# Value products of a banded attention: six of 256 columns in place of four of 512, with values and queries loaded by key head

## Chip, cores and metric

The kernel runs on one core of one Trainium2 chip. The metric is the device time of one execution in microseconds (us). The engines are named as in the profile: PE is TensorE (matrix products; PEld is its loading of weights), DVE is VectorE, ACT is ScalarE, POOL is GpSimd, SP is SyncE, which issues nearly all DMA transfers here. Each engine works through its own instructions in order, and waits where an instruction needs a result of another engine.

## What is computed

One layer of a decoder: an input projection, two branches (attention over a sliding window of 128 keys, and a chunked gating MLP), their merge, and a convolutional FFN. A prompt of 1024 tokens and 8 samples of 8 tokens share the weights. The change concerns the prompt's attention alone:

```python
BLOCK = WINDOW = 128; HEAD_DIM = 64; N_HEADS = 16; N_KV_HEADS = 4; GQA_GROUP = 4
def attn_prompt(q, k, v, sinks):
    ...                                     # blocks of 128 queries; keys of the block before and of the own one
    diff = arange(BLOCK)[:, None] + BLOCK - arange(2 * BLOCK)[None, :]
    band = (diff >= 0) & (diff < WINDOW)
    mask = band[None] & valid[:, None, :]
    o = sink_attention(qb, kk, vv, mask[:, None, None], sinks)   # softmax with a learned sink, then p @ v
```

For query q of a block the band lets in key j of the own block where j <= q, and key j of the block before where j > q. So each query sees 128 keys, one for each j.

## The kernel before

**Numbers in two parts.** Products run in a rounded 32-bit type (fp32r), and an operand x is held as a high part and a low part (`split`: the high part is a rounded copy by ACT, the low part the difference by DVE). A product is then three products, or, where the weights hold both parts side by side, two.

**Tokens in two groups.** Group 0 has the 64 sample tokens and prompt blocks 0 to 3, group 1 prompt blocks 4 to 7. `attention(gr, pieces)` runs for group 0, then for group 1. It has 16 steps, one for each key head `kv` (0 to 3) and block `i` (0 to 3); one step handles the 4 query heads that share the key head, 128 queries each: 512 columns.

**One step** has three parts, which the loop at the end of `attention` puts two steps apart:

- `sc_p`: scores by 8 products `sc` (two for each query head); `s` has 128 slots for each query, slot j holds the score of the key j that the band lets in; maximum, exponential and sum follow on DVE and ACT.
- `tr_p`: four transposes `pt` turn the probabilities over (slots on the partitions, 512 query columns); `ph` and `pl` are their high and low parts. POOL keeps the slots j <= q of each (`affine_select`) as `ch` and `cl`.
- `pv_p`: values. Tile `vst` of a block holds for each key head 64 columns of high and 64 of low parts of v. Four products of 512 columns add up in `po`: v of the block before times `ph` and `pl`, and `dvst` (v of the own block less v of the block before) times `ch` and `cl`, which corrects the slots whose key is in the own block. The very first block of the prompt (b = 0) has no block before it and takes two products only: so of 32 steps 28 have four.

**Work beside the attention.** Between these parts `fill()` calls the next pieces of other work: products `mm` of `branch` (group 0) or `merge` (group 1). They are what PE does while a step's chain of ACT, DVE and POOL runs. A scheduler orders every engine's instructions by priority when the program is built, so the rows of an engine stand near but not exactly in the order of the code.

**Values in DRAM.** Early in the program, `v_out` writes for each block a tile of values (`vd0` to `vd6`) and one of differences (`dvd1` to `dvd7`), 128 x 512 numbers each, from buffers `ws`. `prepare(gr)` returns the loads: per group 3 or 4 tiles `vst` and as many `dvst`, all key heads at once, which `fill()` issues near the beginning of the group's attention; keys `kst` and queries `q` are loaded for each key head by `operands(kv)`.

## Time and profile before

| | |
|---|---|
| median of 3 runs | 1527.02 us (1525.86 to 1528.16) |
| the profiled execution's own time | 1527.68 us |
| its span, first to last instruction | 1526.0 us, so 1.68 us lie around it |
| mean granted TensorE clock | 0.996 of full speed |
| PE, PEld busy | 1512.0 us (99%), 1489.0 us (98%) |
| DVE, ACT, POOL busy | 1152.4 us (76%), 822.6 us (54%), 257.3 us (17%) |
| DMA | 284.05 MB, mean 186 GB/s |

The steps of the prompt's attention lie between about 490 us and 690 us: group 0 up to 600 us, group 1 from there. Busy shares are of the span; products of PE overlap in the records (a record lasts from its start to its modelled end), so the time that one takes on PE is read from the distance between starts. A row of the timeline gives start, duration, engine, line, operation, the tiles written and read, and in square brackets how long the engine sat idle before it and for whom.

### The profile page before, as it was taken

Reading aid. Unit: us, or ns where it says so; the run is one execution under the profiler, and the core shown is the slowest. Engines: PE = TensorE matmul, PEld = TensorE weight load, DVE = VectorE, ACT = ScalarE, POOL = GpSimd, SP = SyncE. Lnnn points to the kernel's source line nnn. Section 1 sums busy time; section 2 is a strip of 40 time slices with the busy share of each in tenths; the row PEclk is TensorE's granted clock in tenths of the full one; section 3 lists DMA queues with packets and bytes.
Section 4 is the critical chain, followed back from the end, with each engine's and each line's share of the span. In section 5 each row is a group of like instructions: output and inputs, shape, how many; then the busy total and the mean of one; then the engine's idle time right before and its main releaser. Section 6 shows DMA issues by size and latency. Waiting matters only on the chain.

```text
span 1526.0 us, 31224 instructions
## 1 busy us (share of the span) xinstructions
PE 1512.0 (99%) x12158; PEld 1489.0 (98%) x12158; DVE 1152.4 (76%) x1910; ACT 822.6 (54%) x1744; POOL 257.3 (17%) x371
## 2 busy tenths in 40 slices
PE   9999999999999999999999999999999999999998
PEld 9999999999998989989999999999999999999997
DVE  6896778766544786888658888898899888785675
ACT  7565764554553675774433555555555556353562
POOL 0000002100020221330122211242232222000003
PEclk9999999999999999999999999999999999999998
DMA  8452458657559646729988432332243226973453
GB/s 289 160 194 89 176 199 263 200 187 246 199 204 297 230 160 208 253 88 307 329 292 279 143 120 97 117 143 97 82 151 111 77 93 217 359 259 96 127 175 132
DMA packets 126819, 284.05 MB, mean 186 GB/s; under 512 B 14800, under 2 KB 32016, under 8 KB 126672
## 3 DMA queue, kind: packets, MB, share of 16 engines
q1 hardware_dynamic: 122640, 278.52, 53.9%
q10 hardware_dynamic: 4032, 3.55, 0.7%
q8 instruction: 95, 1.56, 0.4%
q14 instruction: 52, 0.43, 0.1%
HBM read 193.40 MB, written 90.59 MB: 186 GB/s over the span
## 4 chain that ended last, share of the span: by engine, by line
PE 73%; DVE 4%; issue 3%; ACT 2%; DMA 2%; POOL 1%; POOLq 0%; SPq 0%; DVEq 0%; ACTq 0%
PE st L294 40%; PE mm L235 16%; PE dn L1666 11%; PE sc L1184 2%; PE po L1232 2%; PE pt L1211 1%; POOL x L1731 1%; DVE wl L41 1%; DMA wraw<-wt 1%; PE mx L831 1%; DMA s<-sd 1%; ACT s L1201 1%; ACT wh L40 0%; DVE v L759 0%; PE po L1144 0%
## 5 line engine op out<-in xcount | busy, mean ns | idle before, releaser
L294 PE MATMUL st<-th,wh 128*128 128x256 f32 (+1 forms) x2128 | 610.8, 287 | 1.3 <-ACT kn L277 0.8
L294 PE MATMUL st<-tl,wh 128*128 128x256 f32 (+1 forms) x2128 | 608.6, 286 | 0.0
L294 PE MATMUL st<-th,wl 128*128 128x256 f32 (+1 forms) x2128 | 608.2, 286 | 0.0
L294 PEld LDWEIGHTS st<-th,wh 128*128 128x128 f32 x2128 | 400.0, 188 | 3.0 <-ACT kn L277 1.2
L294 PEld LDWEIGHTS st<-th,wl 128*128 128x128 f32 x2128 | 400.2, 188 | 0.0
L294 PEld LDWEIGHTS st<-tl,wh 128*128 128x128 f32 x2128 | 399.7, 188 | 0.0
L40 ACT CAST wh<-wraw 128x512 fp32r<-128x512 f32 (+2 forms) x204 | 139.6, 694 | 97.3 <-PE st L294 35.2
L41 DVE TENSOR_TENSOR wl<-wraw,wh 128x512 fp32r<-128x512 f32 (+2 forms) x204 | 158.2, 788 | 39.8 <-ACT wh L40 37.4
L1666 PE MATMUL dn<-th,wh 128*128 128x288 f32 (+1 forms) x616 | 176.7, 287 | 0.0
L1666 PE MATMUL dn<-tl,wh 128*128 128x288 f32 (+1 forms) x616 | 176.2, 286 | 0.0
L1666 PE MATMUL dn<-th,wl 128*128 128x288 f32 (+1 forms) x616 | 175.1, 284 | 0.0
L40 ACT CAST wh<-ws 128x512 fp32r<-128x512 f32 x160 | 98.1, 621 | 97.0 <-PE st L294 62.4
L41 DVE TENSOR_TENSOR wl<-ws,wh 128x512 fp32r<-128x512 f32 x160 | 109.7, 698 | 48.9 <-ACT wh L40 47.2
L1666 PEld LDWEIGHTS dn<-th,wl 128*128 128x128 f32 x616 | 115.9, 188 | 0.0
L1666 PEld LDWEIGHTS dn<-tl,wh 128*128 128x128 f32 x616 | 115.7, 188 | 0.0
L1666 PEld LDWEIGHTS dn<-th,wh 128*128 128x128 f32 x616 | 115.6, 188 | 0.0
L282 POOL TENSOR_TENSOR z<-kn,k 128x256 f32<-128x256 f32 (+1 forms) x32 | 29.7, 933 | 315.1 <-ACT kn L277 299.5
L235 PE MATMUL mm<-s,wh 128*128 128x256 f32 (+1 forms) x384 | 78.2, 298 | 1.1 <-DMA s<-sd 1.1
L40 ACT CAST th<-traw 128x544 fp32r<-128x544 f32 (+1 forms) x85 | 54.0, 642 | 45.6 <-PE dn L1666 30.6
L41 DVE TENSOR_TENSOR tl<-traw,th 128x544 fp32r<-128x544 f32 (+1 forms) x85 | 61.5, 731 | 20.8 <-ACT th L40 20.6
L525 PE MATMUL st<-w2h,th 128*128 128x256 f32 x308 | 73.9, 281 | 0.2 <-ACT w2h L40 0.2
L235 PE MATMUL mm<-oh,wh 128*128 128x256 f32 (+1 forms) x256 | 73.7, 288 | 0.0
(288 smaller groups left out, 3154.0 us busy)
## 6 DMA issues: line engine op xcount, KB each, us to landing
wraw<-wt SPq DMA_DIRECT2D x133, 512.0 KB
traw<-td SPq DMA_DIRECT2D x77, 272.0 KB
td<-za SPq DMA_DIRECT2D x22, 544.0 KB
wraw<-wt SPq DMA_DIRECT2D x35, 256.0 KB
upd<-hl SPq DMA_DIRECT2D x14, 512.0 KB
td<-t SPq DMA_DIRECT2D x11, 544.0 KB
qd<-q SPq DMA_DIRECT2D x8, 576.0 KB
q<-qd SPq DMA_DIRECT2D x8, 576.0 KB
```

The source lines that it names most:

```text
L40: S.copy(hi, src)
L41: V.tensor_sub(lo, src, hi.bitcast(F32))
L235: PE.matmul(ps[:, lo:lo + c1 - c0], u[:, k, :], v[:, c0:c1], start=(k == 0 and i == 0), stop=(k == nk - 1 and i == 2))
L282: op(to, pick(x, to, lo, hi), pick(y, to, lo, hi))
L294: PE.matmul(ps, u[:, kk, :], v, start=first and kk + i == 0, stop=kk == 3 and i == 2, skip_group_check=True)
L525: PE.matmul(ps, u, v[:, k, :], start=k + i == 0, stop=k == KD - 1 and i == 2)
L831: PE.matmul(ps[:, P * i:P * i + P], vn[:, i], late["wst"][:, c, :], start=True, stop=True)
L1184: PE.matmul(ps[:, h, o0:256], q, kst[kv][:, e, k0:cur + P], start=e == 0, stop=e == 1)
L1201: S.activation(s[:, h], s[:, h], AF.Exp, bias=nm[:, h:h + 1], accum_out=dn[:, h:h + 1])
L1211: PE.transpose(pt[:, h * P:h * P + P], s[:, h, 0:P], ident)
L1232: PE.matmul(po, v[:, kv, :], t, start=e == 0, stop=e == len(parts) - 1)
L1666: PE.matmul(place(m, e), u[:, m, :], v[:, lo:hi], start=new and i + k == 0 and (e == 0 or m % 2 == 0), stop=i == NU - 1 and k == 2, skip_g ...
```

## The change

For a query in the first half of its block (q < 64) all slots j >= 64 belong to the block before; for one in the second half all slots j < 64 belong to the own block. The new code takes the halves of the queries apart (`half(x, e)`: of each head's 128 columns the 64 of half e, so 4 x 64 = 256 columns). Half 0 starts from v of the block before and is corrected in slots 0 to 63 with `v - z`; half 1 starts from v of the own block and is corrected in slots 64 to 127 with the opposite difference. A correction thus has only 64 slots, and its high part and low part are stacked in one tile `c` of 128 partitions, against `dvst` with the 64 rows of differences twice. A step has then four products of 256 columns with `vst` and two with `dvst`: six of 256 for four of 512. The tile `c` is made by four `affine_select` of 64 partitions x 256 columns, two of which move their rows by 64 partitions.

Values lie in DRAM by key head (`vd`, `dvd`: key head, block, 128 columns); v is now kept for block 7 too. `values(kv)` loads for one key head the blocks of the group: one transfer for `vst` and four of 64 partitions for `dvst`; the call for the next key head stands in `sc_p` at step i = 2, that of `operands` for the next key head at step i = 0 (for the first head it was the last entry of the list before). The store of a block's values writes runs of 512 bytes, and the difference is two instructions of 64 partitions.

```diff
@@ -332,9 +332,9 @@
         kd = [dr(f"kd{c}", [P, 2, T]) for c in range(2)]
         gud = [dr(f"gud{c}", [P, T]) for c in range(NG)]
         sgd = [[dr(f"sg{e}d{c}", [P, T]) for c in range(KD)] for e in range(2)]
-        vd = [dr(f"vd{i}", [P, NKV, P]) for i in range(7)]
+        vd = dr("vd", [P, NKV, 8, P])
         v3d = dr("v3d", [P, 256])
-        dvd = [None, *(dr(f"dvd{i}", [P, NKV, P]) for i in range(1, 8))]
+        dvd = dr("dvd", [P, NKV, 8, P])
         gvd = {name: dr(f"gvd{name}", [P, GW]) for gr in groups for name, _ in gr["toks"]}
         vnd = [dr(f"vnd{gr['g']}", [P, NG, len(gr["toks"]), P]) for gr in groups]
         sd_ = [[dr(f"sd{g}{c}", [P, 2, n]) for c in range(NG)] for g, n in ((0, 576), (1, 512))]
@@ -538,17 +538,18 @@
                         late["v"] = gvp.tile([P, 256], F32, name="gv")
                         nc.sync.dma_start(late["v"], v3d)
                     for to, x in ((vd, v), (dvd, None)):
-                        if (to[name] if name < len(to) else None) is None:
+                        if x is None and name == 0:
                             continue
                         t = W.sm.tile([P, 4, P], F32, name="ws", bufs=2)
                         tr, four = t.bitcast(F32R), lambda y: y.rearrange("p (h d) -> p h d", d=64)
                         if x is None:
                             x = t[:, :, 64:128]
-                            V.tensor_sub(x, four(v), four(late["v"]))
+                            for r, (y, z) in ((0, (v, late["v"])), (64, (late["v"], v))):
+                                V.tensor_sub(x[r:r + 64], four(y)[r:r + 64], four(z)[r:r + 64])
                         else:
                             x = four(x)
                         split(tr[:, :, 0:64], tr[:, :, 64:128], x)
-                        nc.sync.dma_start(to[name], t)
+                        nc.sync.dma_start(to[:, :, name], t)
                     late["v"] = v
                     if name == 3:
                         nc.sync.dma_start(v3d, v)
@@ -933,17 +934,24 @@
                                 nc.sync.dma_start(q.bitcast(F32), qd[g][c])
                     return go
 
-                def value(name, src, i):
+                b0, nv, nd = ((0, 4, 3), (3, 5, 4))[g]
+
+                def values(kv):
+
                     def go():
-                        t = gr[name][i] = kvp.tile([P, NKV, P], F32R, name=f"{name}{i}")
-                        nc.sync.dma_start(t.bitcast(F32), src[i])
+                        if kv < NKV:
+                            v = kvp.tile([P, nv, P], F32R, name="vst", bufs=2)
+                            d = kvp.tile([P, 2, nd, P], F32R, name="dvst", bufs=2)
+                            gr["vst"][kv], gr["dvst"][kv] = v, d
+                            nc.sync.dma_start(v.bitcast(F32), vd[:, kv, b0:b0 + nv])
+                            for e in (0, 64):
+                                for o in (0, 64):
+                                    nc.sync.dma_start(d[o:o + 64, e // 64].bitcast(F32),
+                                                      dvd[e:e + 64, kv, b0 + 1:b0 + 1 + nd])
                     return go
 
-                gr["operands"] = operands
-                vs, ds = (((0, 1, 2), (1, 2, 3)), ((3, 4, 5, 6), (4, 5, 6, 7)))[g]
-                return [operands(0), value("vst", vd, vs[0])] + [
-                    x for i in range(len(ds)) for x in (
-                        [value("vst", vd, vs[i])] * (i > 0) + [value("dvst", dvd, ds[i])])] + [operands(1)]
+                gr["operands"], gr["values"], gr["b0"] = operands, values, b0
+                return [operands(0), values(0)]
 
             done, prep, qko = [], [], ExitStack()
             late["qk"] = poola("qk", 1, qko)
@@ -1070,7 +1078,7 @@
             def attention(gr, pieces):
                 g, n, off, soff = gr["g"], gr["n"], gr["off"], gr["soff"]
                 has_s = soff > 0
-                act, kst, vst, dvst, qt = actp[g], *(gr[x] for x in ("kst", "vst", "dvst", "qt"))
+                act, kst, qt = actp[g], gr["kst"], gr["qt"]
                 if has_s:
                     qs, kn, vs, sp = (smp[x] for x in ("qs", "kn", "vs", "p"))
                 nblk = 4
@@ -1183,8 +1191,10 @@
                             for e in range(2):
                                 PE.matmul(ps[:, h, o0:256], q, kst[kv][:, e, k0:cur + P],
                                           start=e == 0, stop=e == 1)
-                        if i == 0 and kv:
+                        if i == 0:
                             gr["operands"](kv + 1)()
+                        if i == 2:
+                            gr["values"](kv + 1)()
                         s = ap.tile([P, 4, P + 1], F32, name="s", bufs=3)
                         G.tensor_copy(s[:, :, P], late["sinkb"][:, 4 * kv:4 * kv + 4])
                         S.copy(s[:, :, 0:P], ps[:, :, P:256])
@@ -1212,24 +1222,35 @@
                         ph = ap.tile([P, 512], F32R, name="ph")
                         pl = ap.tile([P, 512], F32R, name="pl")
                         split(ph, pl, pt)
-                        b = gr["blk0"] + i
-                        prev = vst[b - 1 if b else 0]
-                        parts = [(prev, ph), (prev, pl)]
-                        if b:
-                            for src, nm in ((ph, "h"), (pl, "l")):
-                                t = ap.tile([P, 512], F32R, name=f"c{nm}")
-                                G.affine_select(t.rearrange("p (h q) -> p h q", h=4),
-                                                src.bitcast(F32).rearrange("p (h q) -> p h q", h=4),
-                                                [[0, 4], [1, P]], ALU.is_ge, 0.0, base=0,
-                                                channel_multiplier=-1)
-                                parts.append((dvst[b], t))
-                        st[kv, i] = parts
+                        parts = []
+                        if gr["blk0"] + i:
+                            c = ap.tile([P, 512], F32R, name="c")
+                            cs, fs, ls = (x.rearrange("p (h e q) -> p h e q", h=4, e=2) for x in (c, ph, pl))
+                            for src, swap in ((fs, 0), (ls, 1)):
+                                for e in range(2):
+                                    r, w = 64 * e, 64 * (e ^ swap)
+                                    G.affine_select(cs[w:w + 64, :, e], src[r:r + 64, :, e].bitcast(F32),
+                                                    [[0, 4], [1 - 2 * e, 64]], ALU.is_ge, 0.0, base=-e,
+                                                    channel_multiplier=2 * e - 1)
+                            parts = [cs]
+                        st[kv, i] = [ph, pl, *parts]
 
                     def pv_p(kv, i):
-                        parts = st.pop((kv, i))
+                        ph, pl, *c = st.pop((kv, i))
                         po = pst.tile([P, 512], F32, name="po")
-                        for e, (v, t) in enumerate(parts):
-                            PE.matmul(po, v[:, kv, :], t, start=e == 0, stop=e == len(parts) - 1)
+                        v, d, b = gr["vst"][kv], gr["dvst"][kv], gr["blk0"] + i - gr["b0"]
+                        if not c:
+                            for e, x in enumerate((ph, pl)):
+                                PE.matmul(po, v[:, 0], x, start=e == 0, stop=e == 1)
+                        else:
+                            half = lambda x, e: x.rearrange("p (h e q) -> p h e q", h=4, e=2)[:, :, e]
+                            for e in range(2):
+                                for x in (ph, pl):
+                                    PE.matmul(half(po, e), v[:, b - 1 + e], half(x, e),
+                                              start=e == 0 and x is ph, stop=False, skip_group_check=True)
+                            for e in range(2):
+                                PE.matmul(half(po, e), d[:, e, b - 1], c[0][:, :, e], start=False, stop=True,
+                                          skip_group_check=True)
                         t = ap.tile([64, 512], F32, name="ot")
                         S.copy(t, po[64:128])
                         of = ap.tile([P, 2, P], F32, name="of", bufs=2)
```

On PE, one step of group 1 (key head 1, block 5, `po` of that step) reads before:

```order
L235 MATMUL mm_8554<-oh1_6443,wh_8341 128x256
L1232 MATMUL po_8451<-ph_8397,vst4_7882 128x512
L235 MATMUL mm_8554<-ol1_6444,wh_8341 128x256
L235 MATMUL mm_8554<-oh1_6443,wl_8342 128x256
L235 MATMUL mm_8554<-oh2_6511,wh_8341 128x256
L1232 MATMUL po_8451<-pl_8398,vst4_7882 128x512
L1232 MATMUL po_8451<-ch_8401,dvst5_7884 128x512
L235 MATMUL mm_8554<-ol2_6512,wh_8341 128x256
L1232 MATMUL po_8451<-cl_8403,dvst5_7884 128x512
L235 MATMUL mm_8554<-oh2_6511,wl_8342 128x256
```

The same step now:

```order
L1249 MATMUL po_8523<-ph_8468,vst_8119 128x4x64
L1192 MATMUL sc_8553<-kst_8275,q_8280 128x256
L235 MATMUL mm_8632<-oh2_6498,wl_8404 128x256
L235 MATMUL mm_8632<-oh2_6498,wh_8403 128x256
L235 MATMUL mm_8632<-ol2_6499,wh_8403 128x256
L235 MATMUL mm_8632<-oh2_6498,wl_8404 128x256
L1249 MATMUL po_8523<-pl_8469,vst_8119 128x4x64
L1249 MATMUL po_8523<-ph_8468,vst_8119 128x4x64
L1249 MATMUL po_8523<-pl_8469,vst_8119 128x4x64
L1252 MATMUL po_8523<-c_8472,dvst_8120 128x4x64 x2
L1221 MATMUL pt_8537<-c_ident_97,s_8436 128x128 x4
```

The first product of a step still stands some products of other work ahead of the second; then five products follow each other, of which the last two read `c`. In the row before, the correction with the high part (`ch`) stood ahead of one `mm`, and the one with the low part (`cl`) behind it.

POOL's rows around the same step before (`s` is the copy of the sinks for a later step):

```order
L1189 COPY s_8494<-c_sinkb_485 128x4
L1221 AFFINE_SELECT ch_8401<-ph_8397 128x512
L1221 AFFINE_SELECT cl_8403<-pl_8398 128x512
L1189 COPY s_8576<-c_sinkb_485 128x4
L1221 AFFINE_SELECT ch_8472<-ph_8468 128x512
```

and now:

```order
L1199 COPY s_8569<-c_sinkb_473 128x4
L1232 AFFINE_SELECT c_8472<-ph_8468 64x4x64 x2
L1232 AFFINE_SELECT c_8472<-pl_8469 64x4x64 x2
L1199 COPY s_8654<-c_sinkb_473 128x4
L1232 AFFINE_SELECT c_8546<-ph_8542 64x4x64 x2
```

Two instructions stand where one stood, in the same place between the copies of the sinks. On SP, the loads at the start of group 1 end before in these rows (`kst`, `q`: keys and queries; `msd` is a store):

```order
L939 DMA dvst6_7888<-dvd6_159 128x512
L939 DMA vst6_7890<-vd6_152 128x512
L939 DMA dvst7_7892<-dvd7_160 128x512
L930 DMA kst_7894<-kd0_122 64x2x640 x2
L933 DMA q_7897<-qd12_114 128x1024
L933 DMA q_7899<-qd13_115 128x1024
```

and now the values of a later head come further down in the group (`wraw` are weights for the other work):

```order
L946 DMA vst_8429<-vd_146 128x640
L949 DMA dvst_8430<-dvd_148 64x512 x4
L931 DMA kst_8562<-kd1_123 64x2x640 x2
L934 DMA q_8565<-qd16_118 128x1024
L934 DMA q_8567<-qd17_119 128x1024
L1287 DMA msd4_176<-stg_8624 128x576
L145 DMA wraw_8842<-wt 128x1024
```

Eight loads of one block each became five of one key head, and the loads for the later heads are spread over the group.

## Prediction

> **What bounds the kernel now.** I read the page first:
>
> ```profile
> span 1526.0 us, 31224 instructions
> PE 1512.0 (99%) x12158; PEld 1489.0 (98%) x12158; DVE 1152.4 (76%) x1910; ACT 822.6 (54%) x1744; POOL 257.3 (17%) x371
> ```
>
> PE is busy for 99% of the span, so time taken off PE shortens the kernel, and a wait added on PE lengthens it, each by its own size. Second, the value products themselves, in the view of their source line:
>
> ```profile
> L1232 PE MATMUL po<-ph,vst x32: 391/397/500, 508.5 to 685.0; 128*128 128x512 f32 x32
> L1232 PE MATMUL po<-ch,dvst x28: 387/393/398, 514.7 to 686.1; 128*128 128x512 f32 x28
> its engine sat idle before it (us, times) until:
>   POOL cl L1221: 6.1, 15
>   DVE pl L41: 1.9, 6
>   ACT ph L40: 0.7, 3
> ```
>
> 28 steps have the four products; the other 4 are untouched. And the last four lines are the ones to look at: PE does stand still here, 8.7 us in all, and 6.1 us of it because POOL's second selection `cl` is not done. POOL is busy for 17% of the span and still ends last in 15 steps. Third, the stage:
>
> ```profile
> 505.00:600.00 95.00, 94.14 (x694) 87.46 (x694) 75.93 (x143) 62.00 (x191) 22.73 (x43) 1.00 0.54 176
> 600.00:690.00 90.00, 88.68 (x635) 82.45 (x635) 74.05 (x142) 63.68 (x199) 24.43 (x45) 1.00 0.59 195
> ```
>
> (busy us of PE, PEld, DVE, ACT, POOL, then granted clock, DMA share, GB/s). The clock is full, DMA has room, DVE is at 80%; throughput is short on PE alone, and what is tight beside it is the order in which a step's results arrive.
>
> **What PE is spared.** A step of group 0 in which PE waits for nothing, and scores of 256 columns (timeline of PE):
>
> ```profile
> 563.10 0.40 PE L1232 MATMUL po<-ph,vst 128*128 128x512 f32 x1
> ...
> 564.02 0.49 PE L1211 MATMUL pt<-c_ident,s 128*128 128x128 f32 x3
> ...
> 565.50 1.12 PE L1184 MATMUL sc<-kst,q 128*128 128x256 f32 x8
> 566.45 0.40 PE L235 MATMUL mm<-s,wh 128*128 128x256 f32 x2
> ```
>
> From start to start, the four products take 0.92 us (0.23 each), and eight of 256 columns 0.95 us (0.119 each). Two of 256 thus cost the same as one of 512, so six cost 0.71 us: 0.21 us less a step, 28 x 0.207 = **5.8 us less on PE**. No row shows a product that reads four runs of 64 columns; I take it at 0.119, as columns are what the rows scale with. If it were 0.14, 28 x 6 x 0.021 = 3.5 us would be lost again; I see no reason that it be below 0.119.
>
> **What POOL is given.** Four selections of 64 partitions x 256 columns replace two of 128 x 512 (groups of POOL by form):
>
> ```profile
> L1221 POOL TENSOR_SCALAR_AFFINE_SELECT cl<-pl 128x512 fp32r<-128x512 f32 x28 | 19.3, 688 | 18.6 <-DVE pl L41 18.6
> L1221 POOL TENSOR_SCALAR_AFFINE_SELECT ch<-ph 128x512 fp32r<-128x512 f32 x28 | 18.0, 642 | 40.7 <-ACT ph L40 40.7
> L1195 POOL TENSOR_SCALAR_AFFINE_SELECT s<-s 128x512 f32<-128x512 f32 x4 | 3.9, 986 | 3.5 <-ACT s L1190 3.5
> L781 POOL TENSOR_SCALAR_AFFINE_SELECT wst<-wst 128x768 f32<-128x768 f32 x1 | 0.9, 870 | 6.8 <-DMA wst<-wst 6.8
> ```
>
> 512 columns take 0.642 us and 768 take 0.870: 0.89 ns a column on a fixed part, so 256 columns come to 0.642 - 0.228 = 0.414 us. Bounds: half of the 512-column one is 0.32, all of it 0.64; half of the `s<-s` one, the only one that walks four separate rows of heads as the new ones do, is 0.49. I take 0.42, next to the line through the two plain rows.
>
> [...]
>
> What matters is not POOL's total but the stretch from the end of `pl` to PE's last product. The step of key head 1, block 5 now:
>
> ```profile
> 635.11 0.64 POOL L1221 TENSOR_SCALAR_AFFINE_SELECT ch<-ph 128x512 fp32r<-128x512 f32 x1 [0.48 <-ACT ph L40]
> 635.64 0.69 DVE L41 TENSOR_TENSOR pl<-pt,ph 128x512 fp32r<-128x512 f32 x1
> 636.40 0.64 POOL L1221 TENSOR_SCALAR_AFFINE_SELECT cl<-pl 128x512 fp32r<-128x512 f32 x1 [0.66 <-DVE pl L41]
> 636.68 0.40 PE L1232 MATMUL po<-pl,vst 128*128 128x512 f32 x1
> 637.27 0.40 PE L1232 MATMUL po<-cl,dvst 128*128 128x512 f32 x1
> ```
>
> `pl` ends at 636.33, `cl` starts 0.07 later and ends at 637.04; 0.05 later PE could use it, at 637.09, and takes it at 637.27: 0.18 to spare. Now: the two selections of `ph` start at 635.11 and end by 635.99, still covered by `pl`. The two of `pl` run 636.40 to 636.82 and, after a gap that I put at 0.04, 636.86 to 637.28; the last is usable at 637.33. PE starts its second product at 636.68 as before, three more follow, and at 636.68 + 4 x 0.119 = 637.16 it wants the last one: it waits 0.17 us. A stop also costs a restart:
>
> ```profile
> 655.88 1.22 DVE L41 TENSOR_TENSOR wl<-wraw,wh 128x1024 fp32r<-128x1024 f32 x1
> 656.03 1.56 POOL L1221 TENSOR_SCALAR_AFFINE_SELECT cl<-pl 128x512 fp32r<-128x512 f32 x1 [0.64 <-DVE pl L41]
> 657.64 0.50 PE L1232 MATMUL po<-cl,dvst 128*128 128x512 f32 x1 [0.74 <-POOL cl L1221]
> 657.98 0.31 PE L235 MATMUL mm<-oh,wl 128*128 128x320 f32 x1
> ```
>
> After the stopped product the next one starts 0.34 us later, not 0.23. So this step loses 0.17 + 0.11 = 0.28. In a step that waits for `cl` already, the restart is paid; there the last selection is usable 0.07 + 0.64 + 0.05 = 0.76 us after `pl` today and 0.07 + 2 x 0.42 + 0.04 + 0.05 = 1.00 then, while PE wants it as early as before (two products of 512, or four of 256, after the one with `pl` starts). It loses **2 x selection - 0.60 = 0.24 us**.
>
> How many steps are that tight? Going through the timeline, in 20 of the 28 `cl` is done less than 0.4 us before its product starts, all 16 of group 1 among them; first and last:
>
> ```profile
> 514.20 0.64 POOL L1221 TENSOR_SCALAR_AFFINE_SELECT cl<-pl 128x512 fp32r<-128x512 f32 x1 [0.18 <-DVE pl L41]
> 514.90 0.49 PE L1232 MATMUL po<-cl,dvst 128*128 128x512 f32 x1
> 685.79 0.76 POOL L1221 TENSOR_SCALAR_AFFINE_SELECT cl<-pl 128x512 fp32r<-128x512 f32 x1 [0.16 <-DVE pl L41]
> 686.60 0.50 PE L1232 MATMUL po<-cl,dvst 128*128 128x512 f32 x1
> ```
>
> In the other 8, such as the one at 563, it is done over 0.7 us ahead, and they lose nothing. 20 x 0.26 = **5.2 us more on PE**.
>
> **What costs nothing, and its cover.** The early part gets 7 more subtractions on DVE, one more split and one more store:
>
> ```profile
> L547 DVE TENSOR_TENSOR ws<-gv x7: 417/419/421, 48.3 to 85.1; 128x256 f32<-128x256 f32 x7
> 102.16 0.75 DVE L41 TENSOR_TENSOR tl<-wh,th 128x576 fp32r<-128x576 f32 x1
> 111.72 0.28 PE L294 MATMUL st<-th,wh 128*128 128x256 f32 x1
> ```
>
> Half the partitions take DVE as long as all, so 8 x 0.42 = 3.4 us; DVE's last operand for the next stage is ready at 102.91 and PE reaches that stage at 111.72, so 8.8 us cover it; without that cover, 3.4. The loads: group 0 has 4 x 5 for 6, group 1 4 x 5 for 8, and SP's issue costs 0.32 us, or 0.55 where 64 rows are cut:
>
> ```profile
> L939 SPq DMA_DIRECT2D vst<-vd x7: 319/320/404, 471.0 to 600.2; - x7
> L930 SPq DMA_DIRECT2D kst<-kd x16: 518/548/661, 466.5 to 636.4; - x16
> ```
>
> 26 more issues are 8 to 14 us of SP in 200, ahead of weight loads (`wraw`) in its queue. The load of a head's values waits until PE is through with the head two before, which is about two steps, 10 us, ahead of use; up to 832 KB at 195 GB/s take 4.3 us. I take both at 0.
>
> **The sum.** -5.8 + 5.2 = -0.6 us. On the profiled execution's own 1527.68 us that is 1527.1; that execution lies 0.66 above the median of the runs, so on the median of 1527.02 it is **1526.4 us**: no change, which I call anything within 0.2% (3.05 us), about what a measurement of this kernel can tell.
>
> **The rivals.**
> - *Selections at half price.* At 0.32 us the tight steps lose 2 x 0.32 - 0.60 = 0.04 each, 0.8 in all: 1522.0 us. For it: half the columns and half the partitions. Against it: 512 and 768 columns show a fixed part. Below 0.37 us the gain passes 3.05 us. Chance 0.25.
> - *The selections grow into the bound, slower.* At 0.55 us a tight step loses 0.50, 10 in all: 1531.2 us; the point from which it is slower is 0.52 (20 x 0.44 = 8.8). For it: the `s<-s` row, and the selection at 656.03, which took 1.56 us beside DVE's subtraction of two SBUF tiles; the second half of the new chain runs where DVE turns from `pl` to such work, and stays there longer. Against it: 642 and 688 as means say that most are left alone. The Trainium skill (GPSIMD Engine Reference, section 1, Specifications) has POOL's SBUF interfaces shared with VectorE, with contention from instructions with two SBUF inputs; the row at 656.03 agrees. Chance 0.27.
> - *A head's values come late.* If five transfers in a queue that waits for PE hold six heads by 1 us each, 1526.4 + 6 = 1532.4 us. Against it: the list of idle time above names no DMA. Chance 0.05.
> - That the change does not do what it says is excluded: the rows of PE show the six products.
>
> **How the numbers follow.** The forecast has 0.43, and I give it 1522.9 to 1529, of which 0.37 is within 0.2%, 0.04 faster and 0.02 slower. Faster: 0.25 + 0.04 = 0.29. Slower: 0.27 + 0.05 + 0.02 = 0.34. Range: from just below the rival at half price, 1521.5, to just above the late values, 1533.0; outside are prices below 0.31 or above 0.59 and the 256-column products at 0.14 on top.
>
> **What would show it.** Right: `po` from start to start 0.119 for six products; selections at 0.42 us; PE idle for `c` near 11 us in about 20 steps, in place of 6.1 for `cl`; nothing else moved. Wrong: a selection under 0.37 or over 0.52 us; products over 0.13 apart without a wait; PE waiting for a DMA of `vst` or `dvst`; stalls of PE before 120 us.

## The result: 10.5 us slower, part of it in a stage where no cost was expected

The changed kernel takes 1537.54 us (median of 5 executions, 1533.39 to 1540.58) against 1527.02 (5 executions, 1524.94 to 1528.16): ratio 1.0071, 95% interval 1.0056 to 1.0085. The forecast was 1526.4, no change, with a range up to 1533.0. The page of an execution that took 1537.54 us:

```profile
span 1535.8 us, 31436 instructions
PE 1512.4 (98%) x12214; PEld 1491.6 (97%) x12214; DVE 1158.1 (75%) x1918; ACT 823.1 (54%) x1745; POOL 276.4 (18%) x427
```

PE's busy time is what it was (1512.0), in a span 9.8 us longer: PE stands still longer. The correction products and the selections, by source line (count, then shortest/median/longest in ns; below, idle us and times):

```profile
L1252 PE MATMUL po<-c,dvst x56: 276/384/391, 516.5 to 693.9; 128*128 128x256 f32 x56
...
  POOL c L1232: 13.2, 29
```

```profile
L1232 POOL TENSOR_SCALAR_AFFINE_SELECT c<-ph x56: 407/413/877, 514.5 to 692.3; 64x256 fp32r<-64x256 f32 x56
L1232 POOL TENSOR_SCALAR_AFFINE_SELECT c<-pl x56: 409/411/1348, 516.0 to 693.4; 64x256 fp32r<-64x256 f32 x56
```

The wait for POOL went from 6.1 us in 15 stops to 13.2 in 29; the forecast had said about 11. Such a list adds the idle time of PE and that of its weight loading (PEld), so one stop can stand in it twice: the 6.1 us are 5.1 of PEld in 13 stops and 1.0 of PE in 2, the 13.2 are 9.2 in 23 and 4.0 in 6. The same two windows of the attention, 4 to 9 us later in the program's time (busy us of PE, PEld, DVE, ACT, POOL, then clock, DMA share, GB/s):

```profile
509.00:604.00 95.00, 91.22 (x710) 87.64 (x709) 75.46 (x140) 61.96 (x190) 29.02 (x67) 1.00 0.60 195
604.00:699.00 95.00, 91.02 (x672) 84.84 (x671) 77.36 (x145) 65.53 (x200) 34.89 (x77) 1.00 0.67 207
```

PE is busy 91.2 of 95 us where it had been 94.1. But attention is not all. A product of PE can be looked up in both traces, since PE's other work is the same; how much later it starts than in the profiled execution of before, worked out from the two start times, tells where time goes:

| product that before starts at (us) | 15 | 95 | 125 | 300 | 455 | 484 | 597 | 740 | 1500 |
|---|---|---|---|---|---|---|---|---|---|
| changed kernel: later by (us) | 0.5 | 0.5 | 3.3 | 4.8 | 4.8 | 2.8 | 3.9 | 9.8 | 9.8 |

So 4.3 us go between 15 and 300 us, where the prediction had put nothing, 2.8 of them at 95 to 125; the 1.5 behind that are followed no further here (threeprod below, whose work up to there is that of before, has 0.7). 2 us come back at 465; attention takes 7.0, 1.1 of it in group 0 and 5.9 in group 1 and behind it; nothing happens after 740.

**The 2 us at 465 are not the change's.** In the profiled execution of before, the granted clock is 0.5 of full speed there for about 3.4 us, and products of 256 columns start 0.21 us apart in place of 0.117 (a window, then rows of PE):

```profile
466.00:467.00 1.00, 1.00 (x6) 1.00 (x6) 0.96 (x4) 0.22 (x1) 0.00 (x0) 0.50 1.25 328
466.40 0.63 PE L235 MATMUL mm<-s,wh 128*128 128x256 f32 x2
466.82 0.41 PE L235 MATMUL mm<-s,wl 128*128 128x256 f32 x1
```

That costs 1.5 us, which the changed kernel, at a full clock there, does not lose; the rest is a wait of PE for a DMA, 1.1 us in before and 0.7 here. Two experiments below whose work up to there is that of before and whose clock is full there (foursel, threeph) gain 2.5 and 2.9 us at the same place, and a third (threeprod), at half clock there itself, gains 0.5. Eleven of the eighteen profiled executions have one or more such stretches ahead of 1500 us, at places that differ, and each costs 1.3 to 1.7 us by the distances between PE's starts. None lies in the attention of before, of the changed kernel, or of oldprod, sixprod, foursel, phsel and best3.

**The early loss.** PE's waits between 98 and 120 us in the changed kernel (us, times, longest), then the rows of the first:

```profile
PE st L294 <- ACT k L275: 2.1, 1, 2.1
PE st L525 <- DVE w2l L41: 0.9, 1, 0.9
```

```profile
100.78 1.22 DVE L41 TENSOR_TENSOR w2l<-wraw,w2h 128x1024 fp32r<-128x1024 f32 x1
...
102.06 0.38 PE L525 MATMUL st<-w2l,th 128*128 128x256 f32 x1 [0.87 <-DVE w2l L41]
```

The low part of a weight is late, because DVE is. The longer wait, at 118 us, is for a copy `k` by ACT, and ACT is late because it had waited 2.0 us for DVE's `ws` (L174), which starts at 109.70, against 102.83 before. In the kernel before, the windows just ahead read:

```profile
80.00:84.00 4.00, 4.00 (x36) 4.00 (x35) 4.00 (x9) 3.73 (x7) 0.00 (x0) 1.00 0.71 242
84.00:88.00 4.00, 4.00 (x36) 4.00 (x35) 4.00 (x8) 2.19 (x6) 0.00 (x0) 1.00 0.88 261
88.00:92.00 4.00, 4.00 (x36) 4.00 (x36) 4.00 (x9) 1.92 (x4) 0.00 (x0) 1.00 0.94 346
92.00:96.00 4.00, 4.00 (x36) 4.00 (x36) 4.00 (x7) 3.86 (x8) 0.00 (x0) 1.00 0.11 39
```

The fourth column group is DVE: 4.00 of 4.00, four times. Here DVE is as full as PE. The same low part was made in before by

```profile
94.78 2.35 DVE L41 TENSOR_TENSOR w2l<-wraw,w2h 128x1024 fp32r<-128x1024 f32 x2
...
100.53 0.28 PE L525 MATMUL st<-w2l,th 128*128 128x256 f32 x1
```

done at 97.13, used at 100.53: 3.4 us of cover, for 3.4 us of added work. By itself the added work would just fit. But in the changed kernel DVE also stands still, where before it did not:

```profile
88.00:92.00 4.00, 4.00 (x36) 4.00 (x36) 2.31 (x5) 0.67 (x1) 0.00 (x0) 1.00 0.94 250
92.13 0.38 ACT L562 ACTIVATE gv<-st 128x256 f32<-128x256 f32 x1 [3.19 <-DMA gvd<-gv]
93.11 0.76 DVE L41 TENSOR_TENSOR tl<-wl,th 128x576 fp32r<-128x576 f32 x1 [2.80 <-ACT th L40]
```

ACT waits 3.2 us for the buffer of a result `gv`, whose store is still on its way; the `th` that DVE needs stands behind it in ACT's queue, and DVE waits 2.8 us. The execution starts 0.5 us late; with 3.4 and 2.8 that makes 6.7 of the 6.9 us by which `ws` is late.

**The attention.** Adding up, between 480 and 710 us, by how much PE's starts lie further apart than usual (108 ns after 128 columns, 117 after 256, 147 after 320, 233 after 512) ahead of each kind of product gives a balance (us; the last three are experiments):

| ahead of | before | changed | oldprod | sixprod | threeprod |
|---|---|---|---|---|---|
| corrections (`c`, or `ch` and `cl`) | 2.6 | 9.4 | 2.4 | 2.5 | 4.8 |
| products with `ph`, `pl` | 1.8 | 3.3 | 2.0 | 4.3 | 2.8 |
| scores | 0.9 | 3.4 | 1.2 | 4.1 | 0.8 |
| transposes | 2.5 | 3.5 | 2.4 | 2.9 | 3.0 |
| all | 10.2 | 22.7 | 10.6 | 17.0 | 15.1 |

12.5 us more of standing still, less 5.8 of products spared, are 6.7 of the 7.0. (About 1.5 us in threeprod's column are a stretch at half clock.)

### The profile page after: what moved, and what is told of

Same layout as the page of the kernel before. It is cut to its first block, busy times and chain, and to the rows that moved or that the text cites. A ratio compares the mean times of both kernels' runs of the same rounds, so it can differ in the third digit from the quotient of the medians.

```text
span 1535.8 us, 31436 instructions
## 1 busy us (share of the span) xinstructions
PE 1512.4 (98%) x12214; PEld 1491.6 (97%) x12214; DVE 1158.1 (75%) x1918; ACT 823.1 (54%) x1745; POOL 276.4 (18%) x427
## 4 chain that ended last, share of the span: by engine, by line
PE 79%; DVE 8%; ACT 5%; DMA 3%; issue 3%; POOL 2%; SPq 0%; POOLq 0%; ACTq 0%; DVEq 0%
PE st L294 48%; PE dn L1687 12%; PE mm L235 12%; PE st L525 2%; ACT s L1211 1%; DVE tl L41 1%; POOL c L1232 1%; DVE wl L41 1%; POOL x L1752 1%; PE sc L1192 1%; PE mx L832 1%; DMA q<-qd 1%; DMA s<-sd 1%; DVE pl L41 1%; ACT wh L40 1%
```

## Experiments

Theory C: the chain from `pl` over POOL to PE loses it. D: the loads. E: the six short products themselves. G: a step has other loops, as long as PE's work. For the early part, A: the stores in runs of 512 bytes; B: DVE's added work. The table gives for each kernel the time (ratio to before with 95% interval) and, by the same products, what it lost in its profiled execution at 95 to 125 us and in attention (484 to 740). A star marks a stage with a stretch of 3.4 us at half clock, two stars one of 6.8 us: about 1.5 us of the figure for each star are the clock's. The median of phsel is that of seven executions; an eighth took 3819 us and is left out.

| run | median, us | ratio | 95 to 125 | attention |
|---|---|---|---|---|
| changed | 1537.5 | 1.0071 (1.0056 to 1.0085) | +2.8 | +7.0 |
| contig | 1535.8 | 1.0064 (1.0049 to 1.0079) | +1.6 | +4.3 |
| onesub | 1535.4 | 1.0057 (1.0045 to 1.0069) | +0.1 | +5.4 |
| early0 | 1534.6 | 1.0058 (1.0045 to 1.0072) | +1.0 | +6.7 |
| signsplit | 1534.2 | 1.0051 (1.0039 to 1.0063) | -0.3 | +6.1 |
| poolsub | 1542.3 | 1.0111 (1.0090 to 1.0132) | +5.8* | +5.2 |
| oldprod | 1528.9 | 1.0016 (1.0007 to 1.0026) | +2.3 | +0.4 |
| sixprod | 1531.8 | 1.0033 (1.0022 to 1.0043) | +4.2* | +0.6 |
| foursel | 1528.8 | 1.0013 (1.0004 to 1.0022) | 0.0 | +3.0 |
| phsel | 1533.8 | 1.0047 (1.0031 to 1.0063) | +6.7** | +1.9 |
| splitsel | 1540.4 | 1.0090 (1.0077 to 1.0103) | +2.4 | +8.7* |
| threeprod | 1524.7 | 0.9988 (0.9976 to 1.0000) | 0.0 | -2.0* |
| threeph | 1523.6 | 0.9984 (0.9969 to 0.9999) | 0.0 | -3.2* |
| defer | 1532.7 | 1.0042 (1.0026 to 1.0059) | +4.6* | +2.0* |
| best | 1536.5 | 1.0066 (1.0049 to 1.0083) | +6.5* | +1.5 |
| best2 | 1529.6 | 1.0022 (1.0013 to 1.0031) | +0.1 | +2.1* |
| best3 | 1529.0 | 1.0015 (1.0004 to 1.0026) | +0.1 | -0.6 |

The times hold such stretches too. Within the executions of one kernel, 0.001 less of mean granted clock, about one stretch, goes with 1.6 us more, and the kernels' means differ: 0.9973 to 0.9975 for the kernel before, 0.9955 for splitsel (four executions), 0.9957 for best, 0.9963 for poolsub and 0.9964 for defer. By that rate, an estimate, some 3 us of the first two times and some 2 us of the last two belong to the clock; whether the edits bring it about is open.

### The parts of the change, one by one

**oldprod**, the new data with the old products (shortened; the loads and the sign of the differences are fitted to them, in number and size as in the changed kernel):

```diff
-                for src, swap in ((fs, 0), (ls, 1)): for e in range(2): G.affine_select(64 partitions, half e)
+                for src, nm in ((ph, "h"), (pl, "l")): G.affine_select(t, src, [[0, 4], [1, P]])
-                six PE.matmul of half(x, e)
+                for e, (y, x) in enumerate(((prev, ph), (prev, pl), (dv, c[0]), (dv, c[1]))):
+                    PE.matmul(po, y, x, start=e == 0, stop=e == 3)
```

> The changed kernel's early part, stores and loads, number and bytes of transfers included, but the four products of 512 columns and two selections of 128x512 of before. Theory C (the new selections are what attention loses by): attention takes what it took before, the early loss of 4.8 us less the 2 us gained at 465 stays, 1530 us. Theory D (attention loses by its loads and by the order they give, at the start of group 1 above all): 1533 us or more, since the products of 256 columns had saved 5.8 us.

1528.9 us: attention +0.4. D falls: as many transfers and bytes, and attention takes what it took before. What is left, 0.16% or 2.4 us, is the early part. All of the attention's loss comes with products and selections.

**sixprod**, on top of oldprod the six products, fed by the two old selections:

```diff
+                for e in range(2):
+                    for x in (ph, pl): PE.matmul(half(po, e), v[:, b - 1 + e], half(x, e))
+                for e in range(2): PE.matmul(half(po, e), d[:, e, b - 1], half(c[e], e))
```

> The kernel with the changed early part and loads and the two old selections of 128x512 (1528.9 us, labelled oldprod), but with the six products of 256 columns: the first correction reads half 0 of ch, the second half 1 of cl (corrections are then incomplete). Theory C: the products give their 28 x 0.207 = 5.8 us, less what PE then waits longer for the same selections (it comes 0.2 us earlier to cl in some 15 steps, 3 us): 1525 to 1526. Theory E: 1529 or more.

1531.8 us, where C asked for 1525 to 1526 and E for 1529 or more. PE has 5.8 us less to do and attention does not get shorter (+0.6, against +0.4 for oldprod). The balance above says where it went, and the idle lists of the scores and of the products with `ph`, `pl` say to whom:

```profile
  DVE s L1202: 1.8, 7
  issue: 1.5, 2
  DMA q<-qd: 1.5, 2
```

```profile
  ACT ph L40: 2.2, 5
  DVE pl L41: 1.9, 7
```

In oldprod the scores wait for DVE 0.4 us in 2 stops, and there is no row for `q`. PE now arrives before the score bank is read out and before `ph` is made; and at the start of group 1 it stops twice ahead of scores, 0.7 and 0.6 us (0.8 each in the weight loading), the second time for queries whose loads are as in oldprod; for the first the profile names nothing ("issue"). Why they come in time there and not here is not settled. In windows of 2 us the DMA share is 0.99 or more from 594 to 612 us in before, and 1.00 or more from 598 to 618 in the changed kernel: the DMA engines are busy without a break there.

**foursel**, the reverse: the kernel before with four selections in place of two.

```diff
-                G.affine_select(t, src, [[0, 4], [1, P]], base=0, channel_multiplier=-1)
+                for e in range(2):
+                    G.affine_select(to[:, :, e], fr[:, :, e], [[0, 4], [1, 64]], base=64 * e, channel_multiplier=-1)
```

> The kernel before, with each of its two selections cut into two of 128 partitions x 256 columns; four products of 512 as before, same order on PE. Theory C (attention loses by the longer chain of POOL): by the prediction's own working 2 x 0.41 - 0.60 = 0.24 us in some 20 tight steps, and what was measured above it in the changed kernel, 5 to 7 us more: 1532 to 1534 us. Theory E (the loss comes from PE taking six shorter products, with two stops at c in a step in place of one): within 2 us of before, 1527 to 1529.

1528.8 us, +2.0 (0.6 to 3.4). C asked for 5 to 7, and E's forecast, within 2 us of before, came true. The longer chain alone costs 2.0 us by the times and 3.0 in the profiled attention, where 5.2 were worked out for it. Its idle list, weight loading included, has 4.3 us more than the 6.1 of before:

```profile
L1223 POOL TENSOR_SCALAR_AFFINE_SELECT cl<-pl x56: 407/416/1336, 511.4 to 685.0; 128x256 fp32r<-128x256 f32 x56
```

```profile
  POOL cl L1223: 10.4, 20
```

128 partitions x 256 columns take 0.416 us, 64 x 256 took 0.411: partitions count for nothing, as the prediction had it.

**phsel**, the changed kernel with `((fs, 0), (fs, 1))` in the loop of selections: four as before, none behind `pl`.

> All four selections read ph, none pl (the low parts of the corrections are then wrong); instructions and columns on POOL are the same, but the chain from pl over POOL to PE is gone: the four have ended about 1.7 us after ph. Theory C (the chain behind pl): the waits of PE for c, 8 to 9 us with their restarts, fall under 2 us, and the time falls by 6 to 7 us to about 1531. Theory D: waits for c fall, other waits take their place, and less than 3 us is gained, 1535 us.

Attention falls from +7.0 to +1.9 in the profiled execution, and the distances ahead of corrections from 9.4 to 5.8; by the ratios the kernel gains 3.7 us, between the 6 to 7 of C and the 3 of D. So C is right as to the place, and some 4 to 5 us of the loss hang on the chain behind `pl`. But with that chain gone, attention is still not below before, though PE has 5.8 us less to do.

**splitsel**, the last selection on DVE beside POOL's third (shortened):

```diff
+                    if e and swap:
+                        V.tensor_mul(cs[w:w + 64, :, e], src[r:r + 64, :, e], above.to_broadcast([64, 4, 64]))
+                        continue
```

> The changed kernel with the last of the four selections (low part of half 1) made on DVE, as a product of pl with a mask of ones and zeros, 64x256; three selections stay on POOL. Behind pl the two then run side by side: c is complete about 0.5 us after pl and not 0.95. Theory C: waits for c fall from 9.4 to about 4 us; DVE has 28 x 0.42 = 12 us more to do in 200 us, of which some comes back as waits: 1532 to 1534 us. Theory F (in attention DVE is as short as POOL): 1537 us or more.

1540.4 us, as F has it: in attention DVE is as short as POOL. (Without its stretch at half clock attention would be near +7, as in the changed kernel, and the two times can hardly be told apart.) The distances ahead of corrections fall to 4.2 us, as C says, and those ahead of products with `ph` rise from 2.3 to 5.9:

```profile
PE po L1258 <- ACT ph L40: 2.4, 1, 2.4
```

DVE is busy 79.7 and 82.1 of 95 us, and ACT's next `ph` waits behind what DVE has not done.

### Does time taken off PE come back as waits?

**threeprod**, the kernel before without one product a step:

```diff
+                        if len(parts) == 4: parts.pop(1)        # (prev, pl)
```

> The kernel before without one of the four products of 512 columns (v of the block before times pl is left out, in 28 steps): 28 x 0.233 = 6.5 us less on PE, about what the six products of 256 spare, with nothing given to POOL or DVE. Theory G (a step's other loops, scores over DVE and ACT and back, are as long as PE's work, so that time taken off PE comes back as waits for ph, for the score bank and for cl): 1525 us or more, stalls of PE in attention up from 10.2 to 15 us or more. Theory H (PE alone binds, and it is the form of the six products that costs): 1520 to 1521 us, stalls unchanged.

6.5 us less on PE, and the kernel is 1.8 us faster (0 to 3.7). H, with 1520 to 1521, falls: a good part of a saving on PE comes back as waits without products of 256 columns and without any change to POOL, DVE or loads. G's bound, 1525, is met within the noise. How much comes back is less sure: attention is 2.0 us shorter here, about 3.5 without its stretch at half clock, and without it the stops are 13.6 us and not G's 15. Line L1234 has the products; who lets PE wait:

```profile
  POOL cl L1221: 7.7, 11
  ACT ph L40: 1.6, 2
  DVE of L1241: 1.4, 2
  POOL ch L1221: 0.9, 3
```

**threeph**: threeprod, and `((ph, "h"), (ph, "l"))` for the two selections.

> The kernel before with three products of 512 for four (the product of pl with v of the block before is left out) and both selections reading ph, so that neither product nor selection waits for pl: 6.5 us less on PE, and no chain behind pl. Theory G1 (what ate the 6.5 us is the chain DVE pl, POOL cl, PE): 1520 to 1521 us. Theory G2 (it is every loop of the step: ph over ACT, the bank of po over DVE, the score bank): 1523 us or more, with waits for ph, for the po bank and for the transposes in place of those for cl.

2.4 us faster (0.2 to 4.7): the side of G2. With the chain behind `pl` cut, 2.4 of the 6.5 us arrive by the times (3.2 in the profiled attention, about 4.7 without its stretch at half clock); transposes now wait 1.6 us for DVE's `s` and 2.1 for ACT's. Which of these loops is the shortest way to the rest is open: every one that was loosened showed the next.

### The early part

**onesub** (one subtraction of 128 partitions), **contig** (stores of 2 KB in a piece; the loads gather) and **early0** (both):

```diff
-                            for r, (y, z) in ((0, (v, late["v"])), (64, (late["v"], v))):
-                                V.tensor_sub(x[r:r + 64], four(y)[r:r + 64], four(z)[r:r + 64])
+                            V.tensor_sub(x, four(v), four(late["v"]))
```

```diff
-        vd = dr("vd", [P, NKV, 8, P])
+        vd = dr("vd", [P, 8, NKV, P])
-                        nc.sync.dma_start(to[:, :, name], t)
+                        nc.sync.dma_start(to[:, name], t)
```

> One subtraction of 128 partitions per block of values where the changed kernel has two of 64 (the sign of the difference is then that of before for all rows, so half of the corrections have the wrong sign). 7 x 0.42 = 2.9 us less on DVE before 100 us. Theory B (DVE's added work uses up the 8.8 us of cover): the stalls at 102 and 118 us shrink by about 3 us together, 1534 us. Theory A (the stores do it): they stay within 1 us, 1537 us.

> Values and differences lie in memory by block again, so that a store writes 2 KB in a piece per partition and the loads gather pieces of 512 bytes; all else is as in the changed kernel. Theory A (the stores in pieces of 512 bytes keep the DMA engines busy at 88 to 92 us, a gelu output waits 3.2 us for its buffer, and PE loses 1.0 us at 102 and 2.2 us at 118): both stalls go, and the time falls by 3 to 4 us to about 1534. Theory B (seven more subtractions on DVE, 3 us, do it): the stalls stay, 1537 us. In both the attention stays as it is, or loses a little where its loads are in smaller pieces.

> The changed kernel's attention with values stored in pieces of 2 KB and one subtraction per block (sign of half the differences wrong): an early part with the work of before but for one store. If the two together make the early loss, no stall at 102 and 118 us, and the time is before + the attention's 5 us: about 1531 to 1532. If the early loss comes from something else (which store comes when), it is 1535 or more.

**signsplit** does onesub with nothing left out: the sign comes in with the split, `scale_split(hi, lo, x, sign)` for `split(hi, lo, x)`.

> The changed kernel with one subtraction per block again, the sign of the lower 64 partitions coming in with the split into high and low parts (scaled copy on ACT, one fused instruction on DVE), so that nothing is left out: 2.9 us less on DVE before 100 us, stores in pieces of 512 bytes stay. Theory B (added work on a full DVE): the stalls at 102 and 118 us fall below 1.5 us together, time 1534 to 1535 us. Theory A (stores): 1537 us.

Six profiled executions of the changed early part (changed, oldprod, phsel, sixprod, splitsel, defer) lost 2.8, 2.3, 6.7, 4.2, 2.4 and 4.6 us at 95 to 125 us. Without the stretches at half clock (by the distances of PE's starts 2.7 us in phsel, 1.5 each in sixprod and defer) it is 2.8, 2.3, 4.0, 2.7, 2.4 and 3.1. With one subtraction, in 512-byte pieces or not, it is 0.1, 1.0, -0.3, 0.1 and 0.1 (onesub, early0, signsplit, best2, best3). So B holds: without the added work on DVE the loss is gone or, in early0, small.

But the added work does not do it alone. Taking the lateness of DVE's `ws` (L174), less what PE was late at 15 us, DVE is 6.4 us behind in the changed kernel and PE loses 2.8; 5.9 and 2.3 in oldprod, 5.9 and 2.4 in splitsel, 5.1 and 1.6 in contig, 3.4 and 1.0 in early0, 2.6 and 0.1 in onesub. So some 2.5 to 3.5 us are covered, near the 3.4 read above. The added work is 3.4; the rest is a stop of DVE, 2.8 us in the changed kernel, 1.7 in contig, and 2.3 of another kind in onesub, where DVE waits for a store of `ws`. onesub shows that a stop alone is covered; that the added work alone would be, or nearly, is worked out and not shown. That the pieces of 512 bytes lengthen the stop, as A has it, fits contig's one profiled execution; it is not shown, for contig's time cannot be told from the changed kernel's. Nor do the times of onesub, early0 and signsplit stand clear of it by themselves.

early0 falls short of its forecast by attention, 6.7 us for 5, and by 1.8 us between 95 and 300. signsplit, best2 and best3, which share the split with a sign, lose another 1.0 to 1.1 us between 15 and 95, ahead of the column, with no wait of PE in the rows; why is open.

**poolsub** makes the two differences on idle POOL (`G.tensor_sub` for `V.tensor_sub`, with contig's stores).

> The changed kernel with values stored in pieces of 2 KB and the differences of values made on POOL, which is idle before 110 us: DVE has then one split more than before (0.4 us) and seven subtractions less (2.9 us). Theory B (DVE is full between 80 and 100 us, and its added work is what delays everything behind it): no stalls at 102 and 118 us, 3 to 4 us less, 1533 to 1534. Theory A': POOL's subtractions take long beside DVE or delay the stores, and the stalls stay, 1536.

1542.3 us, the worst of all. DVE has less to do, but the instructions queued behind a difference wait for it in order:

```profile
L548 POOL TENSOR_TENSOR ws<-gv x14: 730/1160/2367, 48.6 to 97.7; 64x256 f32<-64x256 f32 x14
```

DVE took 0.42 us for each. The Trainium skill (GPSIMD Engine Reference, section 4.1, Engine selection) has POOL about twice as slow as DVE for two inputs. Here, beside a full DVE, it is 2.8 times by the medians, and 5.6 times at worst.

### Can it be mended?

**defer** reads `c` later, behind the next step's transposes and a piece of other work (shortened; `c` gets two buffers):

```diff
+                        if i >= 3: out_p(*steps[i - 3])      # the two products with c, after tr_p and fill
```

> The changed kernel with the two products that read c put behind the next step's transposes and a piece of other work (c in two buffers); nothing is left out. Waits for c should fall from 9.4 to under 3 us. Theory C (waits for c are what is lost): 1530 to 1532 us. Theory G (a step's other loops are as long): the sum is finished later, waits for c turn into waits for ph, the score bank and the transposes, 1534 us or more.

1532.7 us, by the ratios 4.4 less than the changed kernel, and attention at +2.0 for +7.0, with a stretch at half clock in it. The next wait stands in its list, the bank of `po`, which is now held longer, until DVE has read it (`of`):

```profile
PE po L1249 <- DVE of L1266: 3.5, 4, 2.1
PE sc L1192 <- DMA q<-qd: 1.5, 1, 1.5
PE po L1258 <- POOL c L1232: 1.2, 2, 0.6
```

**best** adds poolsub's early part, **best2** contig and signsplit; **best3** is best2 with the products of `c` right behind the transposes:

> The edits of the last two together, the version to which the findings point: by theory C with B 1526 to 1528 us, by theory G 1531 or more.

> Nothing left out: the changed kernel with one subtraction per block and the sign in the split, values stored in pieces of 2 KB, and the products that read c put behind the next step's transposes and a piece of other work. The early loss gone (theory B) and the attention as in the run labelled defer, 2 us above before, less the 2 us gained at 465: 1527 to 1529 us. If the early loss is luck of when a store lands: 1531 to 1532.

> As the run labelled best2, but the products that read c come right behind the next step's transposes, without the other work between, so that the bank of po is free earlier: waits for po's bank (3.5 us in the run labelled defer) go, waits for c come back in part. By theory C 1529 to 1531 (c), by theory G 1527 to 1529 (the bank counts as much as c).

1536.5, 1529.6 and 1529.0 us. best went wrong by poolsub's part. best2 and best3 cannot be told apart by their times, and 1529 is where the forecasts of C and G for best3 meet, so it does not decide between them. In best3 attention is at -0.6, and it waits for the bank and for `c` in about equal parts:

```profile
PE po L1252 <- DVE of L1269: 2.3, 3, 1.4
PE po L1261 <- POOL c L1235: 1.6, 3, 0.7
PE pt L1224 <- DVE pl L41: 0.8, 2, 0.4
```

It regains 8.6 us of the 10.5 by the medians, and is still 0.15% (0.04 to 0.26%) above before. No version here with the six products beats the kernel before.

## Why the prediction was wrong

1. **"PE is busy for 99% of the span, so time taken off PE shortens the kernel, and a wait added on PE lengthens it, each by its own size."** This is the step that failed first. The price was right, as undisturbed rows show, 0.11 to 0.12 us from start to start:

```profile
674.50 0.28 PE L1249 MATMUL po<-pl,vst 128*128 128x256 f32 x1
674.62 0.28 PE L1249 MATMUL po<-ph,vst 128*128 128x256 f32 x1
674.73 0.28 PE L1249 MATMUL po<-pl,vst 128*128 128x256 f32 x1
674.85 0.34 PE L1252 MATMUL po<-c,dvst 128*128 128x256 f32 x1
```

   So PE is spared the 5.8 us. But oldprod to sixprod shows nothing of it in attention, and threeprod gives 1.8 of 6.5 by the times (about 3.5 in its profile without the stretch at half clock). A share of 99% says that PE seldom stands still, not that nothing else is as long: in 10 of the 28 steps before, PE takes `cl` within 0.07 us of its end, and a PE that comes earlier waits. The lines on DVE at 80% and on `cl` ending last (15 stops, which are 13 steps) stood in the prediction, and should have said that PE's arrival cannot be moved forward for free.
2. **"What costs nothing, and its cover": 3.4 us of DVE under a cover of 8.8.** This step failed too: 2.8 us at 95 to 125, 4.3 by 300 us. The cover was read at one consumer, the next stage's operands at 111.72 us; a nearer one was `w2l`, done at 97.13 and used at 100.53, 3.4 us. And nothing was allowed for a stop of DVE itself, which came, 2.8 us for ACT's `th`.
3. **The loads at 0.** Right for the values: no wait for `vst` or `dvst`, and oldprod's attention is that of before. Not foreseen: two stops ahead of scores at the start of group 1, 1.06 and 0.63 us beyond the usual distance in the changed kernel; the profile names the queries' load for the second and nothing for the first.
4. **Selections at 0.42 us, 20 tight steps, +5.2 us.** The median is 0.41, and in 19 of the 28 steps the last correction starts within 0.07 us of the last selection's end. By itself the longer chain costs 2.0 us (foursel; 3.0 in its profile). The idle time that the working started from, 6.1 us of PE, was for the most part that of weight loading; by the distances of its starts PE lost 2.6 us ahead of corrections. In the changed kernel it loses 9.4, so +6.8; the mean of the selections of `pl`, 506 ns, lies above their median because in seven steps the last selection ran into DVE and took 0.66 to 1.35 us:

```profile
516.03 1.70 POOL L1232 TENSOR_SCALAR_AFFINE_SELECT c<-pl 64x256 fp32r<-64x256 f32 x2 [0.61 <-DVE pl L41]
...
516.52 0.93 DVE L41 TENSOR_TENSOR wl<-wraw,wh 128x768 fp32r<-128x768 f32 x1
...
517.78 0.39 PE L1252 MATMUL po<-c,dvst 128*128 128x256 f32 x1 [0.76 <-POOL c L1232]
```

   These two took 1.70 us, where an undisturbed pair takes 0.89. That is the second rival's mechanism, "stays there longer". The Trainium skill (GPSIMD Engine Reference, section 1, Specifications) has POOL's SBUF interfaces shared with VectorE, with contention from DVE instructions with two SBUF inputs; this row agrees. The rival put its price on every selection (0.55) where it falls on a few; its side was right.
5. **The signs it named beforehand** would have told: "stalls of PE before 120 us" came, "nothing else moved" failed, while `po` at 0.119 and the selection at 0.42 came true. The prices of a product, a selection and a subtraction were right (0.117, 0.41 and 0.42 us) and the time was wrong by 11 us: the error lay in what the prices are worth at their places.

By medians: 2.4 us come with the data (oldprod), 2.6 more with the six products (sixprod less oldprod), 5.8 more with the selections on top of them: 10.8, which is what the ratio of the whole gives. The first is uncertain by about 1.5 us, the other two by 2 to 3.

## What to carry to other kernels

A saving on the busiest engine is worth what the next loop lets through: take the work away without replacing it, in one cheap run, and see how much of it arrives, before anything is added to pay for it. Cover has to be read at every consumer behind the added instruction in its queue, and a window in which that engine is busy 4.00 of 4.00 us gives back nothing of what is added. Ahead of comparing two executions stage by stage, the granted clock of each stage has to be read: a stretch at half clock costs 1.5 us here, as much as several of the effects that were looked for. When a product waits at the end of a chain, reading the chain's result later was worth more here (4.4 us) than making the chain shorter on another engine (splitsel gained nothing).

## Seen on the way

The last part of the program, which no version touches, runs at two speeds. Between 1330 and 1480 us products of 256 columns stand mostly 113 to 114 ns apart in the profiled executions of before and best3, and 117 to 118 in those of contig and onesub, with a granted clock of 1.00 in all and no waits; from 1290 to 1500 us contig thus falls back by 3.4 us and onesub by 3.1. That is as much as the bound of 0.2%, in a place where nothing was changed, and a reason to end the comparison of single executions at 740 us, as the table does.
